# The GLU stage of a streaming-encoder step: ScalarE and VectorE in a written order, gates cut into row groups

## The chip, the cores and the metric

The kernel runs on one core of a Trainium2 chip, in one launch. The metric is the device time of one execution in microseconds (us); the text compares medians. Engine names as the profile has them: PE is TensorE (matrix products), PEld its weight loads, DVE is VectorE, ACT is ScalarE, POOL is GpSimd, SP is SyncE, which here only issues DMA transfers.

## The reference

One layer is run on a prompt of 1024 tokens and on 32 further tokens, together NT = 1056 tokens. The parts that the change touches are these:

```python
z = h @ w_in                      # columns: u, zs, q, k, v, za, indexer q, indexer k, weights, gates
ys, hr, hi = ssm_scan(u, ...)     # branch A: a state-space model over u, 512 channels
ys = gelu(ys)
ys = ys * sigmoid(ys @ w_glu + b_glu)
ys = ys * silu(zs)
```

Branch B (a sparse attention whose keys an indexer picks) follows later; both branches are projected, merged, projected again and normalised. All of it is in fp32. The kernel forms each fp32 product from three products of rounded parts: an operand x is split into a high part xH (a cast to fp32r) and a low part xL = x - xH, and the product is wH*xH + wH*xL + wL*xH (`mm3`, L270 to L273).

## The kernel before

**Layout.** Channels lie on the 128 partitions and tokens along the free dimension. Tokens are worked on in three groups of G3 = 352 columns, n = 0, 1, 2. The 512 channels of branch A are four tiles, q = 0 to 3.

**The stream of projections.** A `Job` is one projection of 128 output channels: its weights are loaded by SP (`raw`, L250), cast by ACT (`wh`, L259), and reduced to the low part by DVE (`wl`, L264). For each n PE then makes the steps k, each three matmuls with 352 columns, into a PSUM tile `pz`, of which there are two; an evacuation `ev(n, ps)` reads the tile and so frees it. `Stream.body` splits the next job's weights and loads those of the one after it at n = 0, k = 1 of a job (`ahead`). `run(us)` emits as many steps as `us` holds at 0.483 each, with the evacuations that fall due. PE's order is the order of the program throughout.

**Before the stage.** The state-space part ends, for each q, with a GELU: ACT squares (L981), DVE multiplies (L984), ACT takes the tanh (L987), DVE multiplies again (L990), and SP stores the tile to DRAM (`yD[q]`, L991). This is in a block `manual_schedule(engines={DVE, Activation})`, in which those two engines take their instructions in the order of the program; it is closed before the stage begins. A small tile `sto` with the last states is then written by four stores on SP (L1045).

**The stage.** In the order of the program: the jobs `ki` (72 channels, evacuated by an ACT copy to `zki`, L1074) and `qi0` (evacuated by two ACT casts, L1067 and L1068, and two DVE subtractions, L1069 and L1070) are queued. Then for each q the tile yg[q] is loaded from yD[q] (L1121) and split into ygH[q] (an ACT cast, L70) and ygL[q] (a subtraction, L73). Each of these is two instructions, one of 1024 and one of 32 columns; the source is read with a stride of 133 elements, since yD has the token's place within a chunk of 8 outside. YS = 10 puts ygL of q = 0 and 2 on POOL, of q = 1 and 3 on DVE. A gate z[q] is loaded with its tanh t[q] (L1088, L1089; two buffers for z, one for t), combined over all 1056 columns on DVE (L1090) and multiplied by yg[q] (L1095, two instructions). The gates of q = 0 and 1 are made before the GLU jobs, those of q = 2 and 3 within the last evacuation of the GLU jobs 0 and 1.

The four GLU jobs `glu0` to `glu3` have four steps k per n; step k needs ygH[k] and ygL[k]. Their evacuation is: tanh on ACT (L1104), z = (tanh + 1) * z on DVE (L1105), a split of z into `yo` (ACT cast L70, POOL subtraction L73, three buffers each) and two stores by SP (L1109). After `glu3` come `qi1`, gate jobs and the indexer. There SP loads `kid` (L1174, L1175), two small rows, and a piece of w_mod, `rraw` (L1157), which a PE product (L1162) needs at a fixed place of PE's order.

**What sets the order.** Outside the closed block a planner, with its own costs, orders ACT, DVE, POOL and SP; it may bring an instruction forward past others that are not ready, into the earlier written block too. On the engine itself the order is then fixed: a waiting instruction holds up all behind it. The splits of a job's weights in the stage are brought forward by it.

Of the kernel before, what the change touches and what calls it, by code (L numbers as in the profile page):

```python
# [7 lines left out]
F32 = mybir.dt.float32  # L8
F32R = mybir.dt.float32r
# [3 lines left out]
ALU = mybir.AluOpType  # L13
# [3 lines left out]
T, TS, D = 1024, 32, 1024  # L17
NT = T + TS
G3 = 352
# [19 lines left out]
KA, LA = 5.0, 1.0  # L39
LAG, RS, MS, RM, RB = 4.0, 4.0, 0.008, 14.0, 1  # L40
FA, FF, SW, SA, SB = ((2.0, 1.3), (2.0, 1.3), (2.4, 1.6), (1.5, 1.5)), 0.08, 1.2, 4.0, 1.0
MR, ML, YS, YW, HI, HG, JO, SF = (), 1, 10, 15, 0, 0, 8, (2, 2, 2, 1)
C_U, C_ZS, C_Q, C_K, C_V, C_ZA, C_QI, C_KI, C_GM = 0, 512, 1024, 1536, 2048, 2560, 3072, 3584, 3656
START = """
# [14 lines left out]
def body(nc, tc, I, O, dbg=None):  # L59
# [5 lines left out]
    def f32(ap):  # L65
        return ap.bitcast(F32)

    def split(h, l, src, heng, leng):
        if heng is se:
            se.copy(h, src)  # L70
        else:
            heng.tensor_copy(h, src)
        leng.tensor_sub(l, src, f32(h))  # L73
# [502 lines left out]
    class Stream:  # L576
# [77 lines left out]
        def run(self, us):  # L654
            self.credit += us / self.STEP
            while self.credit >= 1:
                if not self.step():
                    self.tick()
                self.credit -= 1
# [52 lines left out]
    def gate_job(f, heng, leng):  # L712
        def begin():
            tg = stg.tile([128, NT], F32, tag="stg", name="tg")

            def ev(n, ps):
                se.activation(tg[:, ns(n)], ps, AF.Tanh, scale=0.5)  # L717
                if n == 2:
                    sp.dma_start(thD[f], tg)
            return ev  # L720
        return Job(f"g{f}", wcol(C_GM + 128 * f), begin, heng=heng, leng=leng)
# [243 lines left out]
    def chain_out(q, ops, HS, mid):  # L965
        Uq, G2, Tq = ops.Uq, ops.G2, ops.Tq
        Yq = xq.tile([128, 8, NCH], F32, name="Yq", bufs=2)
        for g in range(8):
            k, r = g // 2, slice(64 * (g % 2), 64 * (g % 2) + 64)
            if g % 2 == 0:  # L970
                if g:
                    mid()
                py = ps_s("py")
            o = py[:, 512 * (g % 2):512 * (g % 2) + NCH]
            te.matmul(o, Tq[:, g].rearrange("p m s -> p (m s)"), Uq[:, g], start=True, stop=False)
            te.matmul(o, G2[:, g].rearrange("p m s -> p (m s)"), HS[:, g % 2, g // 2, 0:NCH], start=False, stop=True)
            if g % 2:
                se.copy(Yq[:, g - 1:g + 1], py.rearrange("p (h c) -> p h c", h=2)[:, :, 0:NCH])
        yh = Yq
        a1 = xq.tile([128, 8, NCH], F32, name="a1")  # L980
        se.activation(a1, yh, AF.Square, scale=math.sqrt(0.044715))  # L981

        def inner():
            ve.scalar_tensor_tensor(a1, a1, 1.0, yh, op0=ALU.add, op1=ALU.mult)  # L984

        def tanh():
            se.activation(a1, a1, AF.Tanh, scale=math.sqrt(2.0 / math.pi))  # L987

        def outer():
            ve.scalar_tensor_tensor(yh, a1, 1.0, yh, op0=ALU.add, op1=ALU.mult)  # L990
            sp.dma_start(yD[q].rearrange("(g m) s c -> (m s) g c", m=16), Yq)  # L991
        return inner, tanh, outer

    run = Z.run
# [47 lines left out]
    sto = tp_.tile([64, 128], F32)  # L1042
    ve.tensor_copy(sto, pt[0:64, 0:128])
    for k, n in enumerate(("sre_p", "sim_p", "sre_s", "sim_s")):
        sp.dma_start(O[n].rearrange("o b (k g) p -> (o b k) (g p)", g=2), sto[16 * k:16 * k + 16])  # L1045
    stX.close()
    stP.close()

# [12 lines left out]
    def qijob(j):  # L1061
        def begin():
            qs = QS[j] = [kp.tile([128, NT], F32R, name=f"qis{e}", bufs=2) for e in range(2)]

            def ev(n, ps):
                c = ns(n)
                se.copy(qs[0][0:64, c], ps[0:64])  # L1067
                se.copy(qs[1][64:128, c], ps[64:128])  # L1068
                ve.tensor_sub(qs[0][64:128, c], ps[0:64], f32(qs[0][0:64, c]))  # L1069
                ve.tensor_sub(qs[1][0:64, c], ps[64:128], f32(qs[1][64:128, c]))  # L1070
            return ev
        return Job(f"qi{j}", wcol(C_QI + 128 * j), begin, heng=se, leng=ve)
# [7 lines left out]
    def tok(t):  # L1080
        return ((t[:, 0:1024].rearrange("p (c s) -> p c s", s=8), slice(0, 128)),
                (t[:, 1024:NT].rearrange("p (c s) -> p c s", s=8), slice(129, 133)))

    yg, Z2 = [], []

    def gate_tile(q):
        z2, t2 = (gp.tile([128, NT], F32, name=n, bufs=b) for n, b in (("z2", 2), ("t2", 1)))
        sp.dma_start(z2, zsD[q])  # L1088
        sp.dma_start(t2, ztD[q])  # L1089
        ve.scalar_tensor_tensor(z2, t2, 1.0, z2, op0=ALU.add, op1=ALU.mult)  # L1090
        Z2.append(z2)

    def gate_y(q):
        for v_, c in tok(Z2[q]):
            ve.tensor_mul(v_, v_, yg[q][:, c])  # L1095

    def glu_job(q):
        def begin():
            z2 = Z2[q]

            def ev(n, ps):
                c = ns(n)
                th = stg.tile([128, G3], F32, tag="sth", name="th")
                se.activation(th, ps, AF.Tanh, scale=0.25, bias=bglu[:, q:q + 1])  # L1104
                ve.scalar_tensor_tensor(z2[:, c], th, 1.0, z2[:, c], op0=ALU.add, op1=ALU.mult)  # L1105
                yo = [gp.tile([128, G3], F32R, name=f"yo{h}", bufs=3) for h in range(2)]
                split(yo[0], yo[1], z2[:, c], se, ge)
                for h in range(2):
                    sp.dma_start(ysD[h][q][:, c], f32(yo[h]))  # L1109
                if n == 2 and q < 2:  # L1110
                    gate_tile(q + 2)
                    gate_y(q + 2)
            return ev
        return Job(f"glu{q}", w_glu[:, 128 * q:128 * q + 128], begin, kt=4, heng=se, leng=ve,
                   rhs=lambda n, k: (ygH[k][:, ns(n)], ygL[k][:, ns(n)]))

    for q in range(4):
        if q == 3:
            gate_tile(0)
        yg.append(gp.tile([128, 8, NCH], F32, name=f"yg{q}").rearrange("p s c -> p c s"))  # L1120
        sp.dma_start(yg[q].rearrange("p c s -> p s c"), yD[q])  # L1121
        for (h_, c), (l_, _) in zip(tok(ygH[q]), tok(ygL[q])):
            split(h_, l_, yg[q][:, c], se, (ge, ve)[(YS >> q) & 1])
    w_glu = I["w_glu"].rearrange("o d e -> (o d) e")
    gate_y(0)
    gate_tile(1)
    gate_y(1)
    ckd = I["cache_kidx"].rearrange("a b (k p) d -> p (a b k) d", p=128)
    for hf_ in range(2):
        sp.dma_start(cki[:, :, hf_], ckd)  # L1130
    Z.add(*(glu_job(q) for q in range(4)), qijob(1), *(gate_job(f, se, ve) for f in range(NS, NI - 1)))
    Z.add(qijob(2), qijob(3), gate_job(NI - 1, se, ve), hold=True)
    Z.until("glu3")
    stG.close()


# [776 lines left out]
```

## Time and profile before

| | us |
|---|---|
| three runs: median, lowest, highest | 1049.09, 1048.04, 1054.11 |
| the profiled execution's own time | 1047.89 |
| its span, first to last instruction | 1046.1 |
| PE busy in the span | 990.5 (95%) |
| DVE, ACT, POOL busy | 768.5, 541.5, 257.6 |
| mean granted TensorE clock | 0.991 of full speed |

Times below are microseconds from the start of the span. The stage of the change lies between about 236 and 301 us. A row's bracket tells how long the engine stood idle before it and which operation ended the wait; where several waits are joined the last one is named.

### The profile page before, as it was taken

The numbers are of one execution on the slowest core, as the hardware profiler recorded it, in microseconds if no ns is written. First come the engines' busy times: TensorE is split into PE (matmuls) and PEld (weight loads), VectorE is DVE, ScalarE is ACT, GpSimd is POOL, SyncE is SP. The second block draws the span as 40 slices with busy tenths as digits, with TensorE's granted clock in tenths as the row PEclk, the third lists the DMA queues.
The fourth block names the chain that finished last, engine by engine and source line by source line (L and its number), as shares of the span: only waits on it lengthen the run. The fifth ranks groups of instructions, "written<-read, shape, count | busy, mean of one in ns | idle before, by whom it ended". The sixth has DMA issues, their size and how long they took to land.

```text
span 1046.1 us, 17197 instructions
## 1 busy us (share of the span) xinstructions
PE 990.5 (95%) x6194; PEld 922.9 (88%) x6194; DVE 768.5 (73%) x1752; ACT 541.5 (52%) x1164; POOL 257.6 (25%) x471
## 2 busy tenths in 40 slices
PE   5999999998989999998998999999999999999997
PEld 3799999997978989997998999899898988998786
DVE  4669798995766879989889846656658776786544
ACT  3642345536345656778994246556466555343111
POOL 3202400002340013333314432333332131440000
PEclk9999999999999999999999999999999999999999
DMA  9922722327682123332322342142224632753311
GB/s 305 277 72 83 226 83 63 95 80 232 195 253 87 61 61 91 85 99 79 89 82 82 113 135 72 43 141 63 62 82 136 195 101 81 257 170 133 131 61 61
DMA packets 125329, 126.00 MB, mean 120 GB/s; under 512 B 14400, under 2 KB 104980, under 8 KB 125244
## 3 DMA queue, kind: packets, MB, share of 16 engines
q1 hardware_dynamic: 124864, 124.59, 39.0%
q8 instruction: 49, 0.80, 0.3%
q14 instruction: 36, 0.29, 0.1%
q10 hardware_dynamic: 220, 0.28, 0.1%
q0 software_dynamic: 160, 0.03, 0.0%
HBM read 87.81 MB, written 36.50 MB: 119 GB/s over the span
## 4 chain that ended last, share of the span: by engine, by line
PE 66%; ACT 10%; DVE 10%; issue 6%; DMA 5%; POOL 2%; SPq 1%; POOLq 0%; ACTq 0%; DVEq 0%
PE pz L271 10%; PE pz L272 10%; PE pz L273 10%; ACT junkb L1547 6%; PE pss L1383 3%; PE psm L1882 3%; PE psm L1883 3%; PE psm L1884 3%; DMA wm<-in_w_mod 2%; DVE junk L1549 2%; PE pt L1476 2%; PE pss L273 2%; PE pss L271 2%; PE pss L272 2%; PE pspo L1495 2%
## 5 line engine op out<-in xcount | busy, mean ns | idle before, releaser
L271 PE MATMUL pz<-hH,wh 128*128 128x352 f32 (+1 forms) x776 | 260.9, 336 | 4.7 <-DVE qis L1070 4.3
L273 PE MATMUL pz<-hH,wl 128*128 128x352 f32 (+1 forms) x776 | 251.3, 324 | 0.0
L272 PE MATMUL pz<-hL,wh 128*128 128x352 f32 (+1 forms) x776 | 251.2, 324 | 0.0
L264 POOL TENSOR_TENSOR wl<-raw,wh 128x256 fp32r<-128x256 f32 (+1 forms) x184 | 133.6, 755 | 118.4 <-ACT wh L259 118.1
L271 PEld LDWEIGHTS pz<-hH,wh 128*128 128x128 f32 (+1 forms) x776 | 145.7, 188 | 8.7 <-issue 5.4
L272 PEld LDWEIGHTS pz<-hL,wh 128*128 128x128 f32 (+1 forms) x776 | 145.8, 188 | 1.5
L273 PEld LDWEIGHTS pz<-hH,wl 128*128 128x128 f32 (+1 forms) x776 | 145.4, 187 | 0.4
L1547 ACT ACTIVATE junkb<-sco,thr 128x896 bf16<-128x896 f32 (+3 forms) x128 | 103.6, 809 | 29.0 <-DVE thr L1612 19.2
L271 PE MATMUL pss<-hH,wh 128*128 128x352 f32 x304 | 102.2, 336 | 9.3 <-ACT tg L717 3.6
L273 PE MATMUL pss<-hH,wl 128*128 128x352 f32 x304 | 100.4, 330 | 1.2 <-POOL wl L264 1.2
L272 PE MATMUL pss<-hL,wh 128*128 128x352 f32 x304 | 100.4, 330 | 0.3 <-DVE hL L73 0.2
L1549 DVE TENSOR_SCALAR_CACHE_REDUCE junk<-sco,thr 128x1024 bf16<-128x1024 f32 (+2 forms) x96 | 96.9, 1009 | 2.4
L263 POOL CAST wh<-raw 128x256 fp32r<-128x256 f32 x88 | 34.5, 432 | 182.9 <-PE pz L272 167.8
L1479 DVE TENSOR_TENSOR PL<-pt,PH 128x512 fp32r<-128x512 f32 (+2 forms) x96 | 50.3, 552 | 28.1 <-ACT PH L1478 26.9
L271 PEld LDWEIGHTS pss<-hH,wh 128*128 128x128 f32 x304 | 58.9, 194 | 13.3 <-POOL wl L264 5.5
L1478 ACT CAST PH<-pt 128x512 fp32r<-128x512 f32 (+2 forms) x96 | 43.0, 482 | 43.2 <-PE pt L1476 39.9
L273 PEld LDWEIGHTS pss<-hH,wl 128*128 128x128 f32 x304 | 58.9, 194 | 1.8 <-POOL wl L264 1.8
L272 PEld LDWEIGHTS pss<-hL,wh 128*128 128x128 f32 x304 | 58.9, 194 | 0.8 <-DVE hL L73 0.8
L1220 DVE SCALAR_TENSOR_TENSOR sco<-rl,wi,sco 128x384 f32<-128x384 f32 (+6 forms) x49 | 45.6, 936 | 16.1 <-ACT rl L1215 15.5
L1215 ACT ACTIVATE rl<-pss 128x384 f32<-128x384 f32 (+6 forms) x56 | 41.0, 737 | 30.0 <-PE pss L1213 25.9
L1396 ACT ACTIVATE Sm<-Sm,mx 128x128 f32<-128x128 f32 (+8 forms) x68 | 52.7, 775 | 7.0 <-DVE mx L1389 7.0
L1884 PE MATMUL psm<-o,mL 128*128 128x512 f32 (+1 forms) x136 | 51.7, 381 | 0.0
(411 smaller groups left out, 2238.0 us busy)
## 6 DMA issues: line engine op xcount, KB each, us to landing
raw<-in_w_in SPq DMA_DIRECT2D x44, 512.0 KB
thD<-tg SPq DMA_DIRECT2D x16, 528.0 KB
tgl<-thD SPq DMA_DIRECT2D x16, 528.0 KB
wm<-in_w_mod SPq DMA_DIRECT2D x8, 1024.0 KB
rraw<-in_w_mod SPq DMA_DIRECT2D x4, 1024.0 KB
kd<-kd SPq DMA_DIRECT2D x32, 128.0 KB
xo<-in_x_prompt SPq DMA_DIRECT2D x8, 512.0 KB
rawo<-in_w_o SPq DMA_DIRECT2D x8, 512.0 KB
```

Of the source, the lines that this page charges most:

```text
L264: leng.tensor_sub(wl[:, c], raw[:, c], f32(wh[:, c]))
L271: te.matmul(ps, wh, xh, start=first, stop=False)
L272: te.matmul(ps, wh, xl, start=False, stop=False)
L273: te.matmul(ps, wl, xh, start=False, stop=last)
L1215: se.activation(rl[:m, :nk], ps[:m, :nk], AF.Relu)
L1220: ve.scalar_tensor_tensor(sco[i][:m, :nk], rl[:m, :nk], w, sco[i][:m, :nk], op0=ALU.mult, op1=ALU.add)
L1396: se.activation(P, P, AF.Exp, scale=-1.0, bias=self.mx, accum_out=self.rs)
L1478: se.copy(PH[:, b0:b1_, oc], src)
L1479: ve.tensor_sub(PL[:, b0:b1_, oc], src, f32(PH[:, b0:b1_, oc]))
L1547: se.activation(junkb[:m, :nk], x[:m], AF.Sign, bias=t, accum_out=cnt[:m, k:k + 1])
L1549: ve.tensor_scalar(junk[:m, :nk], x[:m], t, None, op0=ALU.is_lt, op1=ALU.add, accum_out=cnt[:m, k:k + 1])
L1884: te.matmul(ps, ml, wh, start=False, stop=last)
```

## The change

- The last of the four yD stores, and the four stores of `sto`, are issued by ACT instead of SP.
- From the loads of yg to the end of `glu3`, DVE and ACT take their instructions in the order of the program (a second written block). PE was in such an order before; POOL and SP stay with the planner.
- The four yg loads come first. Then the steps of the jobs `ki` and `qi0` are spread between the four splits of yg, by `run` with YR = 3.9, 2.0, 2.0, 5.5, 3.0. All ygL are on DVE.
- The gates are made in three row groups of 352 columns (`gate_part`): the gate of q = 0 ahead of the GLU jobs, that of q + 1 in the evacuations of `glu`q. z and t have two buffers each under new tags, and those of q = 2 and 3 take over the space of yg[0] and yg[1].
- The split of z into `yo` and its stores wait in a list until the tanh of the following step has been emitted (`glu_out`).

```diff
+YR = 3.9, 2.0, 2.0, 5.5, 3.0
-            sp.dma_start(yD[q].rearrange("(g m) s c -> (m s) g c", m=16), Yq)
+            (se if q == 3 else sp).dma_start(yD[q].rearrange("(g m) s c -> (m s) g c", m=16), Yq)
...
-        sp.dma_start(O[n].rearrange("o b (k g) p -> (o b k) (g p)", g=2), sto[16 * k:16 * k + 16])
+        se.dma_start(O[n].rearrange("o b (k g) p -> (o b k) (g p)", g=2), sto[16 * k:16 * k + 16])
...
-    def gate_tile(q):
-        z2, t2 = (gp.tile([128, NT], F32, name=n, bufs=b) for n, b in (("z2", 2), ("t2", 1)))
+    def gate_load(q, tags):
+        z2, t2 = (gp.tile([128, NT], F32, name=n, tag=g, bufs=1) for n, g in zip(("z2", "t2"), tags))
         sp.dma_start(z2, zsD[q])
         sp.dma_start(t2, ztD[q])
-        ve.scalar_tensor_tensor(z2, t2, 1.0, z2, op0=ALU.add, op1=ALU.mult)
...
-    def gate_y(q):
-        for v_, c in tok(Z2[q]):
-            ve.tensor_mul(v_, v_, yg[q][:, c])
+    def gate_part(q, z2, t2, n):
+        c = ns(n)
+        ve.scalar_tensor_tensor(z2[:, c], t2[:, c], 1.0, z2[:, c], op0=ALU.add, op1=ALU.mult)
+        v = lambda a, k: z2[:, a:a + 8 * k].rearrange("p (c s) -> p c s", s=8)
+        k = 44 if n < 2 else 40
+        ve.tensor_mul(v(G3 * n, k), v(G3 * n, k), yg[q][:, 44 * n:44 * n + k])
+        if n == 2:
+            ve.tensor_mul(v(T, 4), v(T, 4), yg[q][:, 129:133])
+    pend = []
+    def glu_out():
+        while pend:
+            yo, z2, q, c = pend.pop(0)
+            split(yo[0], yo[1], z2[:, c], se, ge)
+            for h in range(2):
+                sp.dma_start(ysD[h][q][:, c], f32(yo[h]))
...
+            if q < 2:
+                gates[q + 2] = gate_load(q + 2, (("yg0", "t20"), ("yg1", "t21"))[q])
             def ev(n, ps):
                 se.activation(th, ps, AF.Tanh, scale=0.25, bias=bglu[:, q:q + 1])
+                glu_out()
                 ve.scalar_tensor_tensor(z2[:, c], th, 1.0, z2[:, c], op0=ALU.add, op1=ALU.mult)
-                yo = [gp.tile([128, G3], F32R, name=f"yo{h}", bufs=3) for h in range(2)]
-                split(yo[0], yo[1], z2[:, c], se, ge)
-                for h in range(2):
-                    sp.dma_start(ysD[h][q][:, c], f32(yo[h]))
-                if n == 2 and q < 2:
-                    gate_tile(q + 2)
-                    gate_y(q + 2)
+                pend.append(([gp.tile([128, G3], F32R, name=f"yo{h}", bufs=3) for h in range(2)], z2, q, c))
+                if q == 3 and n == 2:
+                    glu_out()
+                if q < 3:
+                    gate_part(q + 1, *gates[q + 1], n)
...
+    dv_.enter_context(tc.manual_schedule(engines={mybir.EngineType.DVE, mybir.EngineType.Activation}))
+    gates = {}
+    Z.add(*(glu_job(q) for q in range(4)))
+    for q in range(4):
+        run(YR[q])
         for (h_, c), (l_, _) in zip(tok(ygH[q]), tok(ygL[q])):
-            split(h_, l_, yg[q][:, c], se, (ge, ve)[(YS >> q) & 1])
+            split(h_, l_, yg[q][:, c], se, ve)
+        if q == 2:
+            gates[0] = gate_load(0, ("z20", "t20"))
+    gates[1] = gate_load(1, ("z21", "t21"))
...
+    run(YR[4])
+    for n in range(3):
+        gate_part(0, *gates[0], n)
+    Z.add(qijob(1), *(gate_job(f, se, ve) for f in range(NS, NI - 1)))
     Z.until("glu3")
+    dv_.close()
```

By the arithmetic of `run`, the 48 steps of `ki` and `qi0` (24 each) fall so: after 8 steps the first `zki` copy and split 0; after 12, split 1; after 16, the second `zki` copy and split 2; after 27 or 28 the third `zki` copy, the weight split of `glu0` and split 3; after 33 or 34 the evacuation of `qi0`'s n = 0 and the gate of q = 0; the evacuations of n = 1 and 2 follow behind that gate.

## Rows read from the trace of the kernel before

**Rows 1.** The page, first part: busy time in us, its share of the span, and instructions of each engine.

```profile
PE 990.5 (95%) x6194; PEld 922.9 (88%) x6194; DVE 768.5 (73%) x1752; ACT 541.5 (52%) x1164; POOL 257.6 (25%) x471
```

**Rows 2.** Windows of 5 us: length, then busy time (and instructions) of PE, PEld, DVE, ACT and POOL, the granted clock, the mean busy share of the DMA engines, and GB/s.

```profile
255.00:260.00 5.00, 1.79 (x12) 1.50 (x10) 4.99 (x4) 4.93 (x7) 3.41 (x3) 0.90 0.81 248
260.00:265.00 5.00, 3.90 (x13) 3.93 (x14) 4.89 (x7) 0.89 (x2) 0.05 (x1) 0.50 0.31 100
...
290.00:295.00 5.00, 4.21 (x26) 4.21 (x27) 4.96 (x4) 2.43 (x6) 2.93 (x2) 1.00 0.92 276
```

**Rows 3.** PE's timeline, the matmuls before which PE stood idle: start, duration, instruction, and in brackets the idle time and what ended it.

```profile
252.68 0.43 PE L271 MATMUL pz<-hH,wh 128*128 128x352 f32 x1 [0.42 <-ACT zki L1074]
...
261.10 0.63 PE L271 MATMUL pz<-hH,wh 128*128 128x352 f32 x1 [4.31 <-DVE qis L1070]
...
269.97 0.40 PE L271 MATMUL pz<-ygH,wh 128*128 128x352 f32 x1 [0.75 <-DVE qis L1070]
...
290.79 0.43 PE L271 MATMUL pz<-ygH,wh 128*128 128x352 f32 x1 [2.50 <-ACT th L1104]
...
311.48 1.06 PE L1162 MATMUL pg<-rraw,scP 128*32 128x512 f32 x8 [1.47 <-DMA rraw<-in_w_mod]
```

**Rows 4.** The instructions on the tile ygH, the first kind of matmul of the GLU jobs: minimum, median and maximum duration in ns, first and last start.

```profile
L271 PE MATMUL pz<-ygH,wh x48: 318/322/432, 267.2 to 294.3; 128*128 128x352 f32 x48
```

**Rows 5.** PE's timeline: the first matmul of `ki`, that of `qi0` 24 steps later, and that of `qi1` behind the GLU jobs.

```profile
236.69 0.40 PE L271 MATMUL pz<-hH,wh 128*72 128x352 f32 x1
...
248.26 0.32 PE L271 MATMUL pz<-hH,wh 128*128 128x352 f32 x1
...
294.76 0.32 PE L271 MATMUL pz<-hH,wh 128*128 128x352 f32 x1
```

**Rows 6.** SP's timeline: the DMA issues ahead of the stage.

```profile
237.22 0.37 SPq L250 DMA_DIRECT2D raw<-in_w_glu  x1
...
242.13 0.38 SPq L991 DMA_DIRECT2D yD<-Yq  x1
242.61 2.21 SPq L1121 DMA_DIRECT2D yg<-yD  x3
```

**Rows 7.** Windows of 1 us, columns as in Rows 2: the DMA share and GB/s stand last.

```profile
239.00:240.00 1.00, 1.00 (x9) 0.88 (x7) 0.67 (x1) 0.29 (x1) 0.00 (x0) 1.00 0.91 258
...
241.00:242.00 1.00, 1.00 (x8) 0.89 (x7) 1.00 (x1) 0.25 (x1) 0.00 (x0) 1.00 0.00 0
...
243.00:244.00 1.00, 1.00 (x8) 0.89 (x7) 0.00 (x0) 0.00 (x0) 0.00 (x0) 1.00 0.93 278
```

**Rows 8.** ACT's timeline ahead of the stage and in it.

```profile
239.71 1.09 ACT L987 ACTIVATE a<-a 128x1064 f32<-128x1064 f32 x1 [1.33 <-DVE a L984]
240.80 0.45 ACT L1074 COPY zki<-pz 72x352 f32<-72x352 f32 x1
...
249.51 2.25 ACT L70 CAST ygH<-yg 128x1024 fp32r<-128x1024 f32 x2 [4.43 <-DMA yg<-yD]
...
258.70 2.19 ACT L70 CAST ygH<-yg 128x1024 fp32r<-128x1024 f32 x2
```

**Rows 9.** DVE's timeline in the stage.

```profile
252.31 2.85 DVE L264 TENSOR_TENSOR wl<-raw,wh 128x512 fp32r<-128x512 f32 x1 [10.21 <-ACT wh L259]
255.08 4.80 DVE L73 TENSOR_TENSOR ygL<-yg,ygH 128x1024 fp32r<-128x1024 f32 x2
259.90 0.52 DVE L1069 TENSOR_TENSOR qis<-pz,qis 64x352 fp32r<-64x352 f32 x1
...
260.98 1.26 DVE L1090 SCALAR_TENSOR_TENSOR z<-t,z 128x1056 f32<-128x1056 f32 x1
...
265.54 2.16 DVE L73 TENSOR_TENSOR ygL<-yg,ygH 128x1024 fp32r<-128x1024 f32 x2
267.84 0.69 DVE L264 TENSOR_TENSOR wl<-raw,wh 128x512 fp32r<-128x512 f32 x1
...
271.03 0.52 DVE L1105 SCALAR_TENSOR_TENSOR z<-th,z 128x352 f32<-128x352 f32 x1
271.47 2.19 DVE L1095 TENSOR_TENSOR z<-z,yg 128x1024 f32<-128x1024 f32 x2
...
289.93 1.23 DVE L264 TENSOR_TENSOR wl<-raw,wh 128x1024 fp32r<-128x1024 f32 x1 [1.11 <-ACT wh L259]
```

**Rows 10.** One piece of the chain of waits: start, duration, and the transfer that it is.

```profile
242.13 6.53 DMA yD<-Yq
```

**Rows 11.** ACT's queue at the start of the kernel: one issue of a DMA by ACT.

```profile
0.74 0.58 ACTq L141 DMA_DIRECT2D crow<-in_c_sample  x1
```

**Rows 12.** The instructions on the tile yg, the gate's multiplication: four of 1024 columns and four of 32; minimum, median and maximum in ns.

```profile
L1095 DVE TENSOR_TENSOR z<-z,yg x8: 196/1130/2697, 262.3 to 296.2; 128x1024 f32<-128x1024 f32 x4, 128x32 f32<-128x32 f32 x4
```

**Rows 13.** POOL's timeline: one subtraction of the `yo` split, and the last three.

```profile
277.40 0.95 POOL L73 TENSOR_TENSOR yo<-z,yo 128x352 fp32r<-128x352 f32 x1 [1.58 <-ACT yo L70]
...
297.51 3.82 POOL L73 TENSOR_TENSOR yo<-z,yo 128x352 fp32r<-128x352 f32 x3 [3.19 <-ACT yo L70]
```

**Rows 14.** SP's timeline behind the stage.

```profile
301.38 0.44 SPq L1109 DMA_DIRECT2D ysLD<-yo  x1
...
306.12 0.40 SPq L1157 DMA_DIRECT2D rraw<-in_w_mod  x1
```

**Rows 15.** The ACT casts of the weights of the jobs `ki` and `qi0`: minimum, median and maximum in ns, first and last start.

```profile
L259 ACT CAST wh<-raw x2: 674/859/1044, 221.6 to 234.9; 128x576 fp32r<-128x576 f32 x1, 128x1024 fp32r<-128x1024 f32 x1
```

More of the change, by code (lines that the diff above doesn't have):

```diff
@@ L1084, in body @@
     yg, Z2 = [], []
-    def gate_tile(q):
-        z2, t2 = (gp.tile([128, NT], F32, name=n, bufs=b) for n, b in (("z2", 2), ("t2", 1)))
+    def gate_load(q, tags):
+        z2, t2 = (gp.tile([128, NT], F32, name=n, tag=g, bufs=1) for n, g in zip(("z2", "t2"), tags))
         sp.dma_start(z2, zsD[q])
         sp.dma_start(t2, ztD[q])
-        ve.scalar_tensor_tensor(z2, t2, 1.0, z2, op0=ALU.add, op1=ALU.mult)
         Z2.append(z2)
-    def gate_y(q):
-        for v_, c in tok(Z2[q]):
-            ve.tensor_mul(v_, v_, yg[q][:, c])
+        return z2, t2
+    def gate_part(q, z2, t2, n):
[13 more added lines that the diff above has]
+                sp.dma_start(ysD[h][q][:, c], f32(yo[h]))
     def glu_job(q):
@@ L1117, in body @@
     for q in range(4):
-        if q == 3:
-            gate_tile(0)
-        yg.append(gp.tile([128, 8, NCH], F32, name=f"yg{q}").rearrange("p s c -> p c s"))
+        yg.append(gp.tile([128, 8, NCH], F32, name=f"yg{q}", tag=f"yg{q}").rearrange("p s c -> p c s"))
         sp.dma_start(yg[q].rearrange("p c s -> p s c"), yD[q])
-        for (h_, c), (l_, _) in zip(tok(ygH[q]), tok(ygL[q])):
-            split(h_, l_, yg[q][:, c], se, (ge, ve)[(YS >> q) & 1])
[L1124 to L1127, printed above, removed]
+    dv_ = ExitStack()
+    dv_.enter_context(tc.manual_schedule(engines={mybir.EngineType.DVE, mybir.EngineType.Activation}))
+    gates = {}
+    w_glu = I["w_glu"].rearrange("o d e -> (o d) e")
+    Z.add(*(glu_job(q) for q in range(4)))
+    for q in range(4):
+        run(YR[q])
+        for (h_, c), (l_, _) in zip(tok(ygH[q]), tok(ygL[q])):
+            split(h_, l_, yg[q][:, c], se, ve)
+        if q == 2:
+            gates[0] = gate_load(0, ("z20", "t20"))
+    gates[1] = gate_load(1, ("z21", "t21"))
     ckd = I["cache_kidx"].rearrange("a b (k p) d -> p (a b k) d", p=128)
@@ L1130, in body @@
         sp.dma_start(cki[:, :, hf_], ckd)
-    Z.add(*(glu_job(q) for q in range(4)), qijob(1), *(gate_job(f, se, ve) for f in range(NS, NI - 1)))
+    run(YR[4])
+    for n in range(3):
+        gate_part(0, *gates[0], n)
+    Z.add(qijob(1), *(gate_job(f, se, ve) for f in range(NS, NI - 1)))
     Z.add(qijob(2), qijob(3), gate_job(NI - 1, se, ve), hold=True)
     Z.until("glu3")
+    dv_.close()
     stG.close()
```

## The prediction

> **What bounds the kernel now.** I read the page first: PE is busy 95% of the span [rows 1], so only time in which PE stands still or runs slowly can be won. The windows of 5 us then show where: in 255 to 260 PE worked 1.79 of 5 us, and from 260 to 265 its granted clock was 0.50, that is 1.2 instead of 2.4 GHz, right behind that pause; in 290 to 295 it paused too, at clock 1.00 [rows 2]. PE's timeline names the pauses of the stage: 0.42, 4.31, 0.75 and 2.50 us, and 1.47 behind the stage for `rraw` [rows 3].
>
> The half clock has a price from rows. `ki` takes 24 steps from 236.69 to 248.26 [rows 5], 0.482 a step, so one n of eight steps takes 3.86. The last n of `qi0` took from 261.10 [rows 3] to 267.2, where `glu0` begins [rows 4]: 6.10, or 2.24 too much. All losses together are 0.42 + 4.31 + 0.75 + 2.50 + 2.24 + 1.47 = 11.69 us. More than these 1.1% the change can hardly win.
>
> Who is late? The chain passes through the last yD store, 242.13 to 248.66 [rows 10]. On SP that store stands ahead of the yg loads [rows 6]; the weights of `glu0` were issued at 237.22, and SP then waits until VectorE has made the last tile. Meanwhile the DMA engines fall idle: 258 GB/s in the microsecond from 239, none in that from 241 [rows 7]. ACT gets its first yg at 249.51, after 4.43 idle [rows 8]. DVE waits 10.21 for `glu0`'s cast weights, which ACT holds behind that; the evacuation that PE misses at 261.10 comes behind two ygL on DVE (4.80) [rows 9] and the ygH on ACT.
>
> **Part 1, the last store off SP.** The loads of q = 0 to 2 no longer wait for 242.1. A tile is 128 x 1064 x 4 bytes = 545 KB, or 2.0 us at the mean 268 GB/s of the two busy windows [rows 7]. The first can land no earlier than about 240.6 (issue behind 237.6, 2.0, and 1 for the way) and no later than now, 249.5. I take 243, since the idle DMA window at 241 has room for it. The Trainium skill, "DMA: Bandwidth & Descriptors", section "Issuing engines are not separate DMA queues", speaks against the part: whichever engine starts a transfer, the same 16 DMA engines run it, and starting elsewhere saves only the sequencer's time. By that alone the loads would come 0.48 us sooner (242.13 to 242.61), and hardly a microsecond of the sum would stay. The row of 241, with idle engines, speaks for a wait rather than for transfer time.
>
> ACT pays for five issues. One took 0.58 [rows 11], so 2.9 at most, beginning when VectorE's tile is ready at 242.1; ACT was then idle for 4.43 [rows 8], which hides it. Without that cover the first ygH would be up to 2.9 later. ACT's work until yg[3], from 243: three ygH pairs at 2.2, two `zki` at 0.45 and `glu0`'s cast (under 1.04 [rows 15]), ends near 251 to 253.
>
> The store itself is issued at 242.1 to 242.7 and takes 6.53 [rows 10], so yg[3] can't start before about 249.0. With 2.0 for itself it lands at 251.0 at best; two gate loads of equal size may share the way, and half of their 4.0 added gives 253.0, which I take. The upper bound is 258.7, where the last ygH begins today [rows 8].
>
> **Part 2, the written order up to `glu0`.** The order puts ygH[3] (2.2) and ygL[3] (2.16 [rows 9]) ahead of the evacuation of `qi0`'s n = 0, two subtractions of 0.52. PE goes on at 253.0 + 2.2 + 2.16 + 1.05 = 258.4. It would be ready at 261.10 - 4.31 - 0.42 = 256.4, as the 0.42 goes with an earlier `zki`. So 2.0 of waiting stay where 4.31 were. After the 2.50 at 290.79 the clock stayed 1.00 [rows 2, 3], so I let the half clock go too. Next late is DVE: the three parts of the first gate stand ahead of n = 1's evacuation. The combination takes 0.52 for 352 columns (as L1105 [rows 9]); the strided product 0.196 for 32 and 2.05 for 1024 columns (twice the median 1130 is about 196 + 2050; the largest, 2697, was blocked [rows 12]), hence 0.80 for 352. Three parts are 4.0, and 258.4 + 4.0 + 1.05 = 263.45 is the start of `glu0`, against 267.2: 3.75 us sooner. PE alone would be done at 258.4 + 3.86 = 262.3. The 0.75 goes, since no ygL is left behind it.
>
> The four ygL all on DVE cost it two pairs more, 4.3 us, between 243 and 253. Today DVE is idle there for 10.21 [rows 9], which covers them, and POOL no longer blocks it. Splitting a combination in three costs 3 x 0.52 instead of 1.26 [rows 9], 0.3 a gate.
>
> **Part 3, the GLU jobs.** First tanh: 263.45 + 4 x 0.482 = 265.4. From there DVE and POOL set the pace if they work strictly by turns. DVE instructions follow each other 0.08 sooner than their durations end (271.03 to 271.47 at 0.52 [rows 9]). DVE: nine L1105 at 0.44, nine gate parts at 0.52 + 0.80 - 0.08 = 1.24, three weight splits at 0.61 (0.69 less 0.08) and `qi1`'s at 1.14: 18.1 us. POOL: nine subtractions of 0.95 [rows 13] less 0.08: 7.8. The sum, 25.9, gives 291.3, and `qi1` starts at 291.4, against 294.76 [rows 5]: **-3.4**. PE alone needs 48 x 0.482 = 23.1, to 286.6. So nearly 5 us of waits stay in the stage, and some of what part 2 wins is lost again: today `glu0` to `qi1` takes 27.6, then 27.95. ACT, with the split one step behind the tanh, is off this sum: a tanh and a cast for every 2.8 us of DVE and POOL.
>
> POOL's last subtraction ends at 301.33 today [rows 13], and SP's stores wait for it, then `rraw` at 306.12 [rows 14]. With `glu3` 3.4 earlier they move by at least as much, so the 1.47 at 311.48 goes: **-1.47**. The gate loads into the space of yg[0] and yg[1] come one job ahead of their use and are hidden; without that, each would cost its 2.0 on DVE.
>
> **Sum.** 3.4 + 1.47 = 4.9. The profiled execution took 1047.89, 1.20 under the median of the runs; the sum is made against it, 1043.0, and against the median 1049.09 it is **1044.2**, 0.5% faster. Its own bounds: yg[3] at 251.0 lets PE go on at 256.4 and gives 2.0 more; at 255.4 all of the 3.4 is gone. About 1041 to 1047.
>
> **Rivals.**
>
> A. *Everything comes back.* If DVE and POOL overlap without blocking, PE alone sets the loop: `qi1` at 286.6, -8.2 - 1.47, 1039.4; with yg[3] at 251.0 all 11.69 go, 1037.4. For it: the pair of gate products at 271.47 took 2.19, no more than two at the median [rows 9, 12]. Against it: the same weight split took 2.85 at 252.31 and 0.69 at 267.84 [rows 9].
>
> B. *Blocking takes the place of the waits.* Without the 0.08 overlaps the turns cost 9 x (0.52 + 1.32 + 0.95) + 3 x 0.69 + 1.23 = 28.4: `qi1` at 293.9, -0.9 - 1.47, 1046.7; one more block of 2.16 (2.85 against 0.69) gives 1048.9. A split that lags a step puts every POOL subtraction beside a gate product. The Trainium skill, "SBUF — State Buffer", section "Who interferes with whom", calls the port pair that VectorE shares with GpSimd an exclusive lock, the loser stopping fully; the 2.85 agrees, and by that rule A is excluded.
>
> C. *Slower: the fixed order waits for the late tile.* The evacuation of `qi0`'s n = 0 can't pass ygH[3] and ygL[3] any more. PE goes on 5.35 + 0.05 behind the landing of yg[3]. If yg[3] lands at 258.7, that is 264.1, a pause of 7.7, with the half clock behind it: `glu0` at 264.1 + 6.10 = 270.2, `qi1` at 298.1, +3.4, and 1.47 stays: 1052.5. It decides from a landing of about 255.4 (255.4 + 5.4 + 6.10 + 27.95 = 294.8). For it: the store's 6.53 and the loads that share the DMA; against it: DMA engines that are idle by then.
>
> D. *The weights come late, so the change doesn't do what it says.* The ACT casts of `ki` and `qi0` run at 221.6 to 234.9 [rows 15], ahead of the yD store; now they head the second written block. If they stay behind that store, `ki` begins at 242.13 + 0.58 + 1.04 = 243.75 instead of 236.69, and with half a clock once (2.24) `glu0` at 243.75 + 48 x 0.482 + 2.24 = 269.1, `qi1` 2.3 later than today: about 1051.5.
>
> E. *The loads come no earlier in effect.* If the transfers themselves and not SP's wait make yg[0] late, the stage starts 0.48 sooner, the time between two issues [rows 6], and the rest stays as it is: 1048.6. For it: DMA at 258 and 278 GB/s around the gap; against it: none at 241 [rows 7]. It is what the rule named in part 1 gives.
>
> **How the numbers follow.** My forecast 0.45, A 0.12, B 0.18, C 0.12, D 0.08, E 0.05. The predicted time is the first one's, 1044. The range 1038.5 to 1052.5 reaches from within A to the end of C and leaves out some 0.15: A's lower end, C and D together, and a planner that reorders the work behind the stage. Within 1% (1038.6 to 1059.6, about what a measurement of this kernel can tell from no change) lie all cases but the lower third of A: faster 0.06; slower 0.07 for mishaps that no case here prices; same 0.87.
>
> **What would show it.** Part 1: yg loads issued on SP near 238 to 240, the first ygH near 243, ygH[3] at 251 to 255. Part 2: a pause of some 2 us before `qi0`'s n = 2 and clock 1.00 after it; `glu0` near 263.5. Part 3: gate products stretched beside POOL subtractions, pauses before the ygH matmuls waiting for `th`, `qi1` near 291. Behind it no pause for `rraw`. I am wrong if `ki` no longer starts at 236.7, if yg[3] lands after 255, or if new waits stand behind 311.

## The result, and the profile after

| | before | changed |
|---|---|---|
| median of the runs taken for the result, us | 1049.74 (10) | 1044.21 (10) |
| lowest to highest | 1048.04 to 1054.11 | 1041.09 to 1046.27 |
| ratio to before, 95% interval | | 0.9942, 0.9928 to 0.9956 |
| profiled execution's own time | 1047.89 | 1044.31 |
| its span | 1046.1 | 1042.4 |

The changed kernel is 0.6% faster; 1044.2 had been forecast. It was timed twice more among the experiments, in a later series: 1045.87 (0.9960, 0.9939 to 0.9982) and 1046.77 (0.9962, 0.9943 to 0.9981). So it wins 0.4 to 0.6% by the three series, whose intervals together reach from 0.2 to 0.7%.

PE's busy time has not moved, as the first part of the page of the changed kernel shows (compare [rows 1]):

```profile
PE 990.6 (95%) x6194; PEld 923.0 (89%) x6194; DVE 773.9 (74%) x1772; ACT 541.6 (52%) x1164; POOL 250.5 (24%) x467
```

What moved is where PE stands. `ki` begins at 239.05 here and at 236.69 before [rows 5]. These 2.4 us arise in the first 46 us, where no changed instruction lies, and differ from profile to profile of one program; over the last 193 us before `ki` the profiles agree within 0.2 us. So every place of the stage is given below **as a distance from `ki`'s first matmul**, which leaves that out. PE's timeline of the changed kernel, first profile, with the matmuls that begin `ki`, the last n of `qi0`, `glu0` and `qi1`, the third matmul of `qi1`, and the one that needs `rraw` (compare [rows 3, 5]):

```profile
239.05 0.40 PE L272 MATMUL pz<-hH,wh 128*72 128x352 f32 x1
...
259.79 0.40 PE L272 MATMUL pz<-hH,wh 128*128 128x352 f32 x1 [1.33 <-DVE qis L1071]
...
264.91 0.40 PE L272 MATMUL pz<-ygH,wh 128*128 128x352 f32 x1 [1.04 <-ACT qis L1069]
...
291.10 0.33 PE L272 MATMUL pz<-hH,wh 128*128 128x352 f32 x1
...
292.80 0.43 PE L274 MATMUL pz<-hH,wl 128*128 128x352 f32 x1 [1.21 <-DVE wl L265]
...
308.52 1.07 PE L1187 MATMUL pg<-rraw,scP 128*32 128x512 f32 x8 [0.70 <-DMA rraw<-in_w_mod]
```

`qi1` comes 52.05 behind `ki` instead of 58.07. But its third matmul, the first that needs its low weights `wl`, then waits 1.21 us for VectorE's split of them. In the kernel before it does not wait:

```profile
295.08 0.32 PE L273 MATMUL pz<-hH,wl 128*128 128x352 f32 x1
```

So what the stage has gained is read at this third matmul: 53.75 instead of 58.39. The same of the third profile, of the same program (its third matmul of `qi1` is at 292.89, behind a pause of 1.19):

```profile
236.79 0.40 PE L272 MATMUL pz<-hH,wh 128*72 128x352 f32 x1
...
259.20 0.40 PE L272 MATMUL pz<-hH,wh 128*128 128x352 f32 x1 [3.01 <-DVE qis L1071]
...
291.21 0.33 PE L272 MATMUL pz<-hH,wh 128*128 128x352 f32 x1
...
308.98 1.06 PE L1187 MATMUL pg<-rraw,scP 128*32 128x512 f32 x8 [1.05 <-DMA rraw<-in_w_mod]
```

And a window of 5 us of the first profile, then of the third (columns as in [rows 2]):

```profile
260.00:265.00 5.00, 3.96 (x25) 3.70 (x25) 4.77 (x10) 1.05 (x3) 0.00 (x0) 1.00 0.55 138
```

```profile
260.00:265.00 5.00, 5.00 (x23) 5.00 (x22) 4.05 (x8) 0.13 (x1) 0.00 (x0) 0.66 0.40 119
```

One program, two courses: in the third profile the pause is 3.01 and the clock is halved for a part of the window (0.66). All three profiles beside the forecast, in us from `ki`'s first matmul:

| | before | forecast | 1st | 2nd | 3rd |
|---|---|---|---|---|---|
| first ygH | 12.8 | 6.3 | 5.9 | 7.1 | 6.5 |
| last ygH | 22.0 | 16.3 | 15.1 | 17.5 | 16.9 |
| pause before `qi0`'s last n | 4.31 | 2.0 | 1.33 | 3.18 | 3.01 |
| lowest clock of a 5-us window, 255 to 270 | 0.50 | 1.00 | 1.00 | 0.65 | 0.66 |
| `glu0` | 30.5 | 26.8 | 25.9 | 29.6 | 27.9 |
| `qi1` | 58.1 | 54.7 | 52.1 | 56.3 | 54.4 |
| `qi1`'s third matmul | 58.4 | | 53.8 | 58.0 | 56.1 |
| from `glu0` to `qi1` | 27.6 | 27.95 | 26.2 | 26.7 | 26.5 |
| from `glu0` to `qi1`'s third matmul | 27.9 | | 27.9 | 28.3 | 28.2 |
| pause for `rraw` | 1.47 | 0 | 0.70 | 1.20 | 1.05 |

(The second profile is of an execution of 1053.97 us, the longest of its series. Against the third, 2.8 us of that arise ahead of `ki` and 3.5 behind the product that needs `rraw`, so how usual its stage is can't be told.)

Where does the landing of yg[3] vary? Mostly in the yD store. The chain of waits of the first profile, and of the third, from that store to the SP issue that waited for it:

```profile
244.49 5.88 DMA yD<-Yq
250.38 0.03 SPq L1136
```

```profile
242.23 6.89 DMA yD<-Yq
249.13 0.03 SPq L1136
```

It took 5.88, 7.42 and 6.89 in the three profiles, 6.53 before [rows 10]. From the SP issue behind it to the last ygH there are 3.75, 4.52 and 4.50 us more, so another 0.8 of the difference lies in the load itself.

### The profile page after: what moved, and what is told of

The parts are those of the page before. It is cut to its first block, busy times and chain, and to the rows that moved or that the text cites. A ratio compares the mean times of both kernels' runs of the same rounds, so it can differ in the third digit from the quotient of the medians.

```text
span 1042.4 us, 17202 instructions
## 1 busy us (share of the span) xinstructions
PE 990.6 (95%) x6194; PEld 923.0 (89%) x6194; DVE 773.9 (74%) x1772; ACT 541.6 (52%) x1164; POOL 250.5 (24%) x467
## 4 chain that ended last, share of the span: by engine, by line
PE 68%; DVE 10%; ACT 9%; DMA 5%; issue 5%; POOL 1%; SPq 0%; POOLq 0%; ACTq 0%; DVEq 0%
PE pz L272 10%; PE pz L273 10%; PE pz L274 10%; ACT junkb L1572 5%; PE pss L1408 3%; PE psm L1907 3%; PE psm L1908 3%; PE psm L1909 3%; PE pss L272 2%; PE pss L274 2%; PE pss L273 2%; PE pt L1501 2%; DMA wm<-in_w_mod 2%; PE pspo L1520 2%; DVE junk L1574 2%
## 5 line engine op out<-in xcount | busy, mean ns | idle before, releaser
L1240 ACT ACTIVATE rl<-pss 128x384 f32<-128x384 f32 (+6 forms) x56 | 41.2, 738 | 30.5 <-PE pss L1238 27.4
```

Of the source, the lines that this page charges most:

```text
L1240: se.activation(rl[:m, :nk], ps[:m, :nk], AF.Relu)
```

## The experiments

Each was timed in the same series as the kernel before, and each has one profile. Places are again from `ki`'s first matmul; the changed kernel has `qi1` at 52.1 to 56.3, `glu0` to `qi1` in 26.2 to 26.7, so a place by itself can differ by 4 us with no edit at all, a stretch of the GLU jobs by 0.5.

**The stores back on SP** (`u_store`).

```diff
-(se if q == 3 else sp).dma_start(yD[q]...
+sp.dma_start(yD[q]...
-se.dma_start(O[n]...
+sp.dma_start(O[n]...
```

> The changed kernel, with the last yD store and the four sto stores issued by SP again; all else stays. My theory (the queue move is what lets the first yg loads start some 4 us before the store, and the written order then pays for every late tile): the first ygH begins near 249.5 instead of 244.9, yg[3] comes after three other loads behind the store, PE pauses over 5 us before the last n of qi0 and may fall to half clock; 1048 to 1053. Rival (the same DMA engines run the transfers whichever engine issues them, so the move is worth under half a microsecond): 1044 to 1045.

Measured: 1049.14, ratio 0.9985 (0.9969 to 1.0000). ACT's timeline shows the first ygH at the old place and a `zki` copy behind it; PE's timeline shows who waits:

```profile
249.25 4.22 ACT L71 CAST ygH<-yg 128x1024 fp32r<-128x1024 f32 x4 [7.87 <-DMA yg<-yD]
253.36 0.45 ACT L1075 COPY zki<-pz 72x352 f32<-72x352 f32 x1
```

```profile
253.87 0.66 PE L272 MATMUL pz<-hH,wh 128*128 128x352 f32 x1 [5.32 <-ACT zki L1075]
```

The theory holds in size, and the rival (transfer time only) falls. The place was another than expected: the order makes a small copy wait behind the late ygH, and PE pauses before `qi0` as a whole, not before its last n. `qi1` is at 57.0, its third matmul, behind a pause of 1.62 for `wl`, at 59.2. Of the five stores it is yD's that holds the loads up: on SP those of `sto` were issued from 237.81 on without waiting, yD's at 242.26, the first load at 242.74.

**The stores alone** (`s_store`): the kernel before, with the opposite of that edit.

> The kernel before, with only the last yD store and the four sto stores issued by ACT. Theory (the early loads are worth nothing without the written order: the planner's order of DVE and POOL loses them again, as when the written block alone was taken out): the first ygH begins some 4 us earlier than 249.5, but qi1's first matmul stays 57 to 59 us behind ki's (58.07 before), 1048.5 to 1050.5. Rival (the loads were the only late thing): qi1 at 52 to 55 behind ki, 1044 to 1047.

Measured: 1047.00, 0.9969 (0.9952 to 0.9986). `glu0` is at 26.6, as early as with the whole change, but `qi1` at 57.4: the GLU jobs take 30.8. The pause of [rows 3] for `th` is there with the same 2.50, and this time the clock falls behind it:

```profile
288.40 0.43 PE L271 MATMUL pz<-ygH,wh 128*128 128x352 f32 x1 [2.50 <-ACT th L1104]
```

```profile
290.00:295.00 5.00, 5.00 (x23) 5.00 (x22) 4.86 (x5) 2.10 (x4) 1.32 (x1) 0.67 0.72 213
```

`qi1` is where the theory put it. The first ygH is not: it was expected some 4 us before 249.5 and begins at 248.64. SP's timeline has the loads issued early, and ACT's shows why they are used late:

```profile
238.91 1.71 SPq L1121 DMA_DIRECT2D yg<-yD  x3
```

```profile
248.11 0.62 ACT L259 CAST wh<-raw 128x512 fp32r<-128x512 f32 x1 [3.22 <-PE pz L272]
248.64 2.25 ACT L70 CAST ygH<-yg 128x1024 fp32r<-128x1024 f32 x2
```

The planner puts the first ygH on ACT behind `glu0`'s weight cast, and ACT stands idle for 3.22 us waiting for PE before it. In the changed kernel 4.3 us pass from the issue of the loads to the first ygH, here 9.7. So it is ACT's order that loses the early loads first, which the theory had put down to DVE and POOL. The time is 1.5 under its range: behind the stage no pause for `rraw` is left in this profile, with its product at 72.6 instead of 74.8.

**No second written block** (`u_order`): the line with `manual_schedule` is taken out, so that the planner orders ACT and DVE.

> The changed kernel without the second written block: the planner orders ACT and DVE again; stores, ygL, row groups and the lagging split stay as changed. Theory (both parts are needed, since the planner puts ygL and ygH pairs ahead of the evacuation that PE misses): half or more of the gain is lost, 1046 to 1050. Rival (the early loads alone bring the gain, the order of the two engines adds nothing): 1043 to 1045.

Measured: 1048.53, 0.9987 (0.9968 to 1.0005). `glu0` at 26.9, `qi1` at 58.6, 31.7 for the GLU jobs, with PE's timeline showing

```profile
280.91 0.66 PE L272 MATMUL pz<-ygH,wh 128*128 128x352 f32 x1 [3.44 <-ACT th L1122]
```

Here too the loads are early and the first ygH is late, at 248.28 and so 12.1 behind `ki`.

At `qi1`'s third matmul, the order without the stores' move is at 59.2, the move without the order at 57.7, all but the order at 58.9; before it is at 58.4, and with the whole change at 53.8 to 58.0. From `glu0` to that matmul the two runs with early loads and without the order take 31.1 and 32.1, `u_store` and the changed kernel 27.9 to 28.3. Early loads start `glu0` sooner, and only the written order keeps that gain through the GLU jobs.

The times say less. With one of the two parts missing the ratios are 0.9985 and 0.9987, worse than each of the changed kernel's three (0.9942, 0.9960, 0.9962), though the intervals overlap those of the two later series. The stores alone reach 0.9969 (0.9952 to 0.9986), which is not clear of these two at all. So how much the rest of the change adds to the moved stores is not settled by the times.

**ygL of q = 0 and 2 on POOL** (`u_pool`).

> The changed kernel with ygL of q = 0 and 2 on POOL again. Theory (DVE has room until yg[3] lands, so moving ygL was worth nothing by itself; blocking between POOL and DVE costs at most one instruction): 1044 to 1046. Rival (POOL holds up DVE's weight split and the third ygL, so PE starts glu0 later): 1046 to 1049.

Measured: 1046.48, 0.9958 (0.9938 to 0.9979); `qi1` at 54.2, as in the third profile of the change. The time is 0.5 beyond the theory's range and in the rival's, but within the changed kernel's three series (1044.2 to 1046.8). Moving ygL was worth nothing that can be seen.

**Whole gates** (`u_rows`): the three parts are made one behind the other at n = 2.

> The changed kernel with the gate of q + 1 made whole, in three parts one behind the other, in the last evacuation of each GLU job. Theory (the sum of DVE's and POOL's work sets the loop, and it stays the same): qi1's first matmul 52 to 53 us behind ki's (52.05 with the change), 1044 to 1045.5. Rival (an evacuation behind 4 us of gate holds PE, which has two PSUM tiles of 1.93 us of work each): one pause of 1 to 3 us in each of glu1, glu2 and glu3, qi1 at 54 to 58, 1046 to 1050.

Measured: 1048.41, 0.9981 (0.9962 to 1.0000). The theory falls, the rival holds: `glu0` to `qi1` takes 29.0. PE's timeline has one pause each at the start of `glu2`, `glu3` and `qi1`, a job later than the rival had them, and what it names is the weight split that DVE has behind the 4 us of gate:

```profile
277.78 0.43 PE L274 MATMUL pz<-ygH,wl 128*128 128x352 f32 x1 [1.10 <-DVE wl L265]
...
286.03 0.43 PE L274 MATMUL pz<-ygH,wl 128*128 128x352 f32 x1 [2.23 <-DVE wl L265]
...
294.96 0.43 PE L274 MATMUL pz<-hH,wl 128*128 128x352 f32 x1 [1.37 <-DVE wl L265]
```

Behind the pause of 2.23 the clock fell as well, to 0.71 in the window from 285 to 290; that is part of the 29.0.

**No lag of the splits** (`u_pend`): `glu_out()` right behind the append, the call ahead of the multiplication taken out.

> The changed kernel with the split of z right behind its multiplication again, not a step later. Theory (strict turns: one more POOL subtraction stands ahead of qi1's weights, and ACT's cast and next tanh, 1.0 us, fit beside the gate part): qi1 52.5 to 53.5 us behind ki, 1044.5 to 1045.5. Rival (ACT's tanh waits behind the cast for VectorE, and PE for the tanh, at each of twelve evacuations): qi1 at 55 or more, 1047 or more.

Measured: 1045.89, 0.9963 (0.9945 to 0.9980); `glu0` to `qi1` in 29.1, 2.4 to 2.9 more than with the lag, and `qi1` at 56.8. Its third matmul doesn't wait and is 29.5 behind `glu0`, 1.2 to 1.6 more than with the lag. PE pauses for `th` seven times, for example:

```profile
281.87 0.43 PE L272 MATMUL pz<-ygH,wh 128*128 128x352 f32 x1 [0.79 <-ACT th L1122]
...
290.32 0.43 PE L272 MATMUL pz<-ygH,wh 128*128 128x352 f32 x1 [1.21 <-ACT th L1122]
```

The stage speaks for the rival. The total doesn't tell the two apart: it lies between the three series of the changed kernel. That the lag is worth 1.2 to 1.6 us in the stage rests on one profile, and no time shows it.

**`yo` on DVE** (`yo_dve`): the test of the turns.

```diff
-            split(yo[0], yo[1], z2[:, c], se, ge)
+            split(yo[0], yo[1], z2[:, c], se, ve)
```

> The changed kernel with the low part of yo subtracted on DVE instead of POOL, which leaves POOL without work in the stage. Theory (DVE and POOL take strict turns, so what counts is the sum of their work: nine subtractions of 0.87 go, nine of 0.44 come, 25.9 becomes 22.0 and PE's own 23.1 sets the loop): glu0's first matmul to qi1's first takes 23.2 to 25 us instead of 27.4, and the time is 1040 to 1042.5. Rival (the engines overlap, POOL's work is free and DVE is the bound): 4 us more on DVE, 1044.5 to 1048.

Measured: 1043.69, 0.9932 (0.9911 to 0.9952); `glu0` to `qi1` in 24.8. Eight of the subtractions stand on DVE ahead of `qi1`'s weight split, 3.5 us more of DVE work at 0.44 each; and yet the stretch is 1.4 to 1.8 shorter, and to `qi1`'s third matmul (25.5) it is 2.4 to 2.8 shorter. (The expectation's 27.4 for the changed kernel is in none of its profiles, which have 26.2 to 26.7.) The time lies between the two expected ranges. The instructions that write z from `th`, all twelve, with minimum, median and maximum in ns, before, changed and here:

```profile
L1105 DVE SCALAR_TENSOR_TENSOR z<-th,z x12: 510/524/1267, 271.0 to 298.4; 128x352 f32<-128x352 f32 x12
```

```profile
L1124 DVE SCALAR_TENSOR_TENSOR z<-th,z x12: 514/1262/1280, 267.7 to 295.9; 128x352 f32<-128x352 f32 x12
```

```profile
L1124 DVE SCALAR_TENSOR_TENSOR z<-th,z x12: 516/520/533, 269.8 to 296.3; 128x352 f32<-128x352 f32 x12
```

In the first profile of the changed kernel seven of the twelve take about 1270: a subtraction of POOL has started shortly ahead of such an instruction (277.17 against 277.73, for one) and is waited out. In the third profile it is five of the twelve (median 523, longest 1300). With POOL empty none takes more than 533. POOL's instructions grow too, from 0.95 [rows 13] to

```profile
277.17 1.46 POOL L74 TENSOR_TENSOR yo<-z,yo 128x352 fp32r<-128x352 f32 x1 [1.75 <-ACT yo L71]
279.65 1.44 POOL L74 TENSOR_TENSOR yo<-z,yo 128x352 fp32r<-128x352 f32 x1 [1.02 <-ACT yo L71]
```

in the changed kernel. The turns are shown; rival A (no blocking) falls. The Trainium skill, "SBUF — State Buffer", section "Who interferes with whom", has this as an exclusive lock; the medians of 1262 and 520 ns agree.

**The evacuations of `qi0` first** (`x_gate`).

```diff
-YR = 3.9, 2.0, 2.0, 5.5, 3.0
+YR = 3.9, 2.0, 2.0, 8.9, 4.9
...
-    for n in range(3):
-        gate_part(0, *gates[0], n)
+    gate_part(0, *gates[0], 0)
+    gate_part(0, *gates[0], 1)
+    run(3.0)
+    gate_part(0, *gates[0], 2)
```

> The changed kernel with the evacuations of qi0 ahead of the last split and of the first gate's second and third part, low part of yo on POOL as in the change. Theory (the pause goes whatever the landing; then DVE's and POOL's turns set the loop from a glu0 that starts earlier): last n of qi0 19.3 behind ki, glu0 at 23.1 to 24, qi1 at 49.5 to 51 (52.05); 1041 to 1043. Rival (the loop gives it all back): qi1 at 52 or more, 1044.

Measured: 1042.42, 0.9920 (0.9902 to 0.9938). The pause is gone (last n at 19.5), `glu0` at 23.3, `qi1` at 51.5, 0.5 outside the expected places: the GLU jobs take 28.2, and 29.9 to `qi1`'s third matmul, so a part is given back. That is as expected where the turns set the pace: DVE is busy for 4.93 us of each 5 from 265 to 285.

**Both of these** (`x_all`).

> The changed kernel with three further edits: the evacuation of qi0's n = 0 ahead of the split of yg[3], those of n = 1 and n = 2 ahead of the second and third part of the first gate in place of behind all three, and the low part of yo on DVE. Theory (the fixed order made PE wait for ygL[3] and for the gate; then DVE's and POOL's turns set the loop): no pause before the last n of qi0, which begins 19.3 to 19.8 us behind ki (20.74 with the change), glu0 at 23.2 to 24 (25.86), qi1 at 47 to 49 (52.05); 1039.5 to 1042. Rival (yg[3] lands too late for glu0's fourth step, so that the pause only moves behind glu0's start): glu0 at 23.2, but qi1 at 50 or more, 1042 to 1044.

Measured: 1041.06, 0.9901 (0.9874 to 0.9928), the best of all and better than the changed kernel's 1044.2 to 1046.8. Last n at 19.2, `glu0` at 23.1, but `qi1` at 50.2, not 47 to 49: the rival's place, though not for the rival's reason. DVE's timeline names a wait that neither theory had, for a buffer of `yo` whose store had not landed, and PE's a pause behind it (in the changed kernel POOL has such a wait already, 1.96 us before its subtraction at 283.04):

```profile
279.51 0.53 DVE L74 TENSOR_TENSOR yo<-z,yo 128x352 fp32r<-128x352 f32 x1 [1.38 <-DMA ysLD<-yo]
```

```profile
281.50 0.43 PE L272 MATMUL pz<-ygH,wh 128*128 128x352 f32 x1 [1.46 <-ACT th L1122]
```

**That wait away** (`x_yo`): the low part is written over z, the high part has six buffers.

> As x_all, with the low part of yo written over z instead of into a buffer of its own, and six buffers for the high part in place of three. In x_all DVE waited 1.38 us for the store that frees a buffer of yo, and PE paused 1.46 and 0.89 behind it. Theory (that wait was all that kept the loop from PE's own pace): no wait of DVE for a store of yo, qi1 47.3 to 48.5 us behind ki (50.15), 1038.5 to 1040.5. Rival (DVE is busy to its limit without the wait too, so PE still pauses): qi1 at 49.5 or more, 1040.5 to 1042.

Measured: 1043.80, 0.9933 (0.9911 to 0.9956). In the stage it does what it should: no such wait, pauses of 0.79 and 0.90 left in the GLU jobs, `qi1` at 48.7, 0.2 beyond the expected places. Then it is lost again, as PE's timeline shows, and the view of waits of SP's queue from 290 to 305:

```profile
306.28 1.93 PE L1189 MATMUL pg<-rraw,scP 128*32 128x512 f32 x8 [5.02 <-DMA rraw<-in_w_mod]
```

```profile
SPq L1201 <- DMA ysLD<-z: 4.2, 1, 4.2
```

SP's load of `kid` now waits 4.2 us for the last store out of z, and `rraw` is queued behind it on SP. Behind PE's pause the clock was 0.50 from 305 to 310, so that the product's eight matmuls took 1.93 instead of 1.06. That `kid` lies over z in memory is what I conclude from the wait; another place for it wasn't tried.

**The changed kernel again** (`again`, `again2`).

> The changed kernel unaltered, for a second profile. In four experiments with the same instructions up to glu0 (ygL on POOL apart) the last ygH began 16.5 to 17.0 us behind ki's first matmul, in the first profile of the change 15.14. Theory (the landing of yg[3] varies from execution to execution, and the first profile was an early one): last ygH at 16.3 to 17.0 behind ki, the last n of qi0 at 22.0 to 22.6 (20.74), a pause of 2.4 to 3.2 us with or without half a clock behind it, glu0 at 27.2 to 29. Rival (the experiments differ by something in their own edits): 15.1 and 20.7 again. Time 1043 to 1046.

> The changed kernel a third time, for one more profile of the same program. Theory (the landing of yg[3] varies): last ygH at 15.1 to 17.0 us behind ki, and the pause before the last n of qi0 longer by what it is later; half the clock behind pauses of over 2 us in some profiles. Rival: the same place as in the first profile, within 0.3 us. Time 1043 to 1046.

Measured: 1045.87 and 1046.77, with the profiles in the table above. By its last ygH, which waits for it in all three, the landing of yg[3] varies by 2.3 us between executions of one program, and the first profile was the earliest of the three; the last ygH of the second, at 17.5, is beyond both expected ranges.

## Why the prediction was right or wrong

**The number** was right, 1044.2 against 1044.21 and at most 2.6 more in the later series, and that it was hit to a hundredth is luck. The product that needs `rraw` was put 4.9 us earlier than before [rows 3, 5]; it came 5.3, 0.6 and 2.6 earlier in the three profiles of the one program, and errors in both directions, told below, cancel in part.

**Part 1 held.** The first ygH was expected 6.3 behind `ki`, measured 5.9 to 7.1. Rival E (1048.6) falls: the first use of the loads gained 5.8 to 6.9 us, because SP no longer waits for VectorE's last tile ahead of them, and `u_store` takes that away again. What the part doesn't say is that it needs part 2 for it: with the loads as early but ACT in the planner's order the first ygH was at 12.1 (`s_store`, `u_order`). The Trainium skill, "DMA: Bandwidth & Descriptors", section "Issuing engines are not separate DMA queues", lets only the sequencer's time be saved by another issuer; for a queue in which a store waits for an engine, the trace differs, by these 5.8 to 6.9 us.

**Part 2 held in its chain and not in one term.** The last ygH was put at 16.3, measured 15.1 to 17.5. What failed is "so I let the half clock go too". It went in the first profile alone. In the other two the store took 7.42 and 6.89 where the working had 6.53, the pause was 3.18 and 3.01, and the clock was halved behind it. So `glu0` came later: at 29.6 and 27.9 instead of 26.8. Nor was 2.50 at full clock a safe sign for a pause of 2.0: behind 1.62 in `u_store` the clock was halved (last section). That is a mild form of rival C, a fixed order that waits for the late tile, without reaching its 1052.5.

**Part 3 held in its sum and not in where it ends.** `glu0` to `qi1` was put at 27.95 and took 26.2 to 26.7. The working adds up DVE's and POOL's work to the end of `qi1`'s weight split and lets `qi1` begin there. But its first two matmuls don't need that split; the third does, and from `glu0` to it 27.9, 28.3 and 28.2 were measured. DVE's timeline of the first profile, its first z and `qi1`'s weight split, and POOL's subtraction just ahead of that split, the ninth of the stage as the working had it:

```profile
267.69 0.53 DVE L1124 SCALAR_TENSOR_TENSOR z<-th,z 128x352 f32<-128x352 f32 x1 [1.06 <-ACT th L1122]
...
291.53 1.22 DVE L265 TENSOR_TENSOR wl<-raw,wh 128x1024 fp32r<-128x1024 f32 x1
```

```profile
290.14 1.39 POOL L74 TENSOR_TENSOR yo<-z,yo 128x352 fp32r<-128x352 f32 x1 [1.02 <-ACT yo L71]
```

From 267.69 to the end of that split are 25.1 us, where the sum was 25.9; but the first z came 2.8 behind `glu0`, not 1.93, since its tanh (0.55) comes first. These two errors cancel. So the GLU jobs did not become faster: to `qi1`'s third matmul they take 27.9 to 28.3, against 27.9 before, about as the working had it (0.35 slower). The expectation that row groups and lag cost nothing either way, which the sum implies, fell with `u_rows` and came into doubt with `u_pend`: not only the sum of DVE's and POOL's work counts but also what stands behind which part of it.

**The term "-1.47" for `rraw` was wrong.** The text let the pause go because SP's stores move by as much as `glu3`. But PE arrives earlier by as much as well, so a pause stays unless SP gains more than PE. Measured 0.70, 1.20 and 1.05: the change gave 0.3 to 0.8 here.

**Rivals.** A falls with the stretched instructions, 1270 against 520 ns. B, blocking in place of the waits, is the right mechanism and in the sum already; its price of 28.4 was not reached (25.1). C occurs in part. D didn't happen: `ki` still starts unhindered, at the same distance from what precedes it, within 0.2 us.

## What to carry to other kernels

Ask of a queue not only how long its transfers take but what stands in it waiting for an engine; a store that must wait belongs on the queue of an engine that would wait anyhow. Early data pays only as far as the next fixed order lets it through: here the loads were issued as early without the written order, and were first used 5 to 6 us later. When two engines take turns, the slower one's work is the first to move, even onto the engine that seems full; and when a chain moves earlier, ask whether its reader moves as well before writing off the pause between them. A stage's gain is read behind the last wait that it can cause, not at the first instruction of the next job.

## What was not expected of the hardware

The clock does not follow from the length of the pause alone. It was halved behind pauses of 1.62 (`u_store`), 2.23 (`u_rows`), 2.50 (`s_store`), 2.71 (`yo_dve`) and 3.01, and stayed at full speed behind 1.74 (`x_gate`), 2.50 before [rows 2, 3], 2.85 (`u_order`) and 3.20 (`u_pend`). The shortest pause with a fall behind it, on PE's timeline of `u_store`, and its window:

```profile
296.05 0.43 PE L274 MATMUL pz<-hH,wl 128*128 128x352 f32 x1 [1.62 <-DVE wl L265]
```

```profile
295.00:300.00 5.00, 3.95 (x15) 3.95 (x16) 3.89 (x5) 2.26 (x4) 2.09 (x2) 0.66 0.56 145
```

And the longest without one, the windows around that of `u_pend`:

```profile
255.00:260.00 5.00, 1.80 (x11) 1.54 (x10) 4.39 (x7) 2.25 (x6) 0.00 (x0) 1.00 1.08 350
260.00:265.00 5.00, 3.95 (x26) 3.69 (x25) 4.77 (x11) 1.51 (x3) 0.00 (x0) 1.00 0.39 122
```

No run here shows what decides it.
